# A decoder trunk on one core: the attention scores of a head group in one run, and two chunks of the output projection woven by K blocks

## The chip, the cores and the metric

The kernel runs on one core of a Trainium2 chip. The core has a matrix engine (TensorE, PE in the profile; its weight loads are PEld), VectorE (DVE), ScalarE (ACT), GpSimd (POOL) and SyncE (SP), which here issues most of the DMAs. Each engine works through its own list of instructions, and semaphores make one wait for another. The metric is the device time of one execution in microseconds (us), the median of several runs.

## What is computed

Two layers over 256 tokens with 2048 channels in float32: a Mamba-2 mixer and a SwiGLU network, then differential attention and a second SwiGLU network. The change is in the attention alone. For each of 16 heads there are two score matrices from 64 channels each; their softmaxes are subtracted, the result weighs the values, and the weighted rows are normalized (the sub-norm):

```python
s = jnp.einsum('bhcqd,bhcsd->bhcqs', q_blk, k).astype(jnp.float32)
s = jnp.where(key_pos[None, :] <= q_pos[:, None], s, -jnp.inf)
pr = jax.nn.softmax(s, axis=-1)
pr = pr[:, :, 0] - lam * pr[:, :, 1]
return jnp.einsum('bhqs,bhsd->bqhd', pr.astype(v.dtype), v)
...
o = rmsnorm(o, subln_w) * (1.0 - lambda_init)
return o.reshape(bsz, s_len, D_MODEL) @ w_out
```

## The kernel before

The 256 tokens are two blocks of 128 (t = 0 and 1). Every large product runs on float32 operands split in two parts: a rounded part (hi) and the rest (lo), and three matmuls hi·hi, hi·lo, lo·hi are summed in PSUM. Weights come in blocks of 512 by 512 (1 MB) by DMA from SP into three buffers; `prep` (L130) makes hi by a cast on ACT (L137) and lo by a subtraction on DVE (L138), into four buffers each. So a block's weights can only be split when the block four before it has been used by PE.

Two forms of product occur here. `mv` (L181) holds the activations in the array and streams the weights: for a chunk of 512 output columns it takes four K blocks, each in two halves; a half gives six matmuls for block t = 0 at once and six for t = 1 a little later (they wait in a list, `lag` halves deep). After each half it calls `tick` (L166). `ws` (L205) holds the weights and gives transposed outputs; it is used for queries and keys, and ticks as well.

Small work is put between these products by `later(k, fn)` (L159): fn is emitted at the k-th tick from now. So the work of attention for one head group runs inside the products of the next one. The emitted instructions are then put in an order for each engine by a scheduler, which may move an instruction past others; what it made of both kernels is shown with the change.

`attention_group` (L982) runs for four groups of four heads. It projects the values with `mv`, queries and keys with `ws`. The evacuation `qk_evac` adds two PSUM parts on ACT (L1004) and DVE (L1005), and scales the keys by the norm (L1008, DVE); a key or query tile of 128 columns by two heads is called qk. Then it puts seven pieces of work in the list: three softmaxes (block 0 with all four heads; block 1 with heads 0 and 1; block 1 with heads 2 and 3), three turns (transposes of the weights, L1052, tile pp, copied to prT), and two weightings (L1063, tile po), and last the pieces: two sets of transposes (tile pt_o) that make the operand of the output projection.

A softmax begins with its scores (L1025): for each head one matmul for each half c of 64 rows, into the PSUM tiles sc0 and sc1. They come from the pool aux, which has four banks. DVE masks the diagonal part (L1030), takes the maximum (L1032) and scales it (L1033); ACT takes the exponentials and their sums (L1036, tile e); DVE then divides: a reciprocal (L1038), e1 by its sum times -lambda (L1040), and e0 by its sum plus that (L1042). The weighting squares its rows on ACT (L1067), sums them (L1069, DVE), adds epsilon (L94, DVE), takes the power -1/2 on POOL (L97) and scales the rows (L1071, DVE, tile ob).

`out_proj` (L686) multiplies by the output weights, four chunks n of 512 columns with `mv`; K block k of each chunk needs head group k. `lookup` (L171) empties the list of put-off work when a group's rows are asked for that aren't there yet. PSUM sums (tile acc) come from a second pool with four banks.

Of the kernel before, what the change touches and what calls it, by code (L numbers as in the profile page):

```python
# [10 lines left out]
F32 = mybir.dt.float32  # L11
F32R = mybir.dt.float32r
AF = mybir.ActivationFunctionType
ALU = mybir.AluOpType
AX = mybir.AxisListType

P = 128
# [8 lines left out]
EPS = 1e-6  # L26
# [4 lines left out]
LAG2 = 2  # L31
# [14 lines left out]
def trunk_kernel(ctx, tc, x_rows, x_cols, vec_cols, vec64, post_rows, lam_rows,  # L46
# [19 lines left out]
    def aux(name):  # L66
        return auxp.tile([P, 512], F32, tag="aux", name=name)
# [5 lines left out]
    o = 0  # L73
# [105 lines left out]


    def mv(blocks, stat, evac, lag, scale=None, loaded=()):  # L181
        acc = {}
        last = 2 * len(blocks) - 1

        def run(i, t, hi, lo):
            if i == 0:
                acc[t] = accp.tile([P, 512], F32, tag="acc", name="acc")
            for j in range(2):
                xh, xl = stat(i, j, t)
                for q, (a, b) in enumerate(((xh, hi), (xh, lo), (xl, hi))):  # L190
                    nc.tensor.matmul(acc[t], a, b[:, j], start=(i == 0 and j == 0 and q == 0),  # L191
                                     stop=(i == last and j == 1 and q == 2))
            if i == last:
                evac(t, acc[t])

        for b, src in enumerate(blocks):
            raw = loaded[b] if b < len(loaded) else None
            sc = scale(2 * b) + scale(2 * b + 1) if scale else None
            for i, (hi, lo) in enumerate(halves(src, sc, raw), 2 * b):
                run(i, 0, hi, lo)  # L200
                pending.append(lambda i=i, hi=hi, lo=lo: run(i, 1, hi, lo))
                flush(lag)
                tick()

# [478 lines left out]
        if not final:  # L683
            later(5, stats)

    def out_proj(w, first, last, acts, kgs, step, final, lag, t512, pw, scale=None, ns=range(4), two={}, forms=None, md=None, mid=None):  # L686

        def sums(t, n):
            mt = m[(t, n)]
            row_sumsq(ss4[t][:, n:n + 1], mt, t512("junk"))
            dst = t512("mw") if n == 3 else mt
            (nc.vector if n == 3 else nc.gpsimd).tensor_tensor(dst, mt, pw(n), op=ALU.mult)
            return dst

        up = sorted(kgs)

        def stat(kg, j, t):  # L700
            hi, lo = lookup(acts, (t, kg // 2))
            return hi[:, kg % 2 * 2 + j], lo[:, kg % 2 * 2 + j]

        def up_stat(i, j, t):
            return stat(up[i], j, t)

        def row(t, e):
            if t not in ss4:
                ss4[t] = small.tile([P, 4], F32, tag="ss4", name="ss_m", bufs=3)
            if e not in summed[t]:  # L710
                summed[t].add(e)
                return sums(t, e)

        ss4 = {}
        summed = {t: set() for t in range(NT)}
        if last:
            pw(0)
            if two:
                pw(1)
        for n, seven in two.items():  # L720
            def done(t, c, ps, ss, n=n):
                y, op = ss[(t, c)]
                k = (t, n + 1 - c)
                nc.vector.tensor_tensor(y, ps, y, op=op)  # L724

                dst = None if last else md[t][:, (n + 1 - c) * 512:(n + 2 - c) * 512]
                if last:
                    nc.vector.tensor_tensor(m[k], m[k], y, op=ALU.add)
                elif first:
                    nc.sync.dma_start(dst, y)  # L730
                else:
                    nc.gpsimd.dma_start(dst, y, accum_op=ALU.add)

            pair([[w[n + e, kg // 2][:, kg % 2 * 2:kg % 2 * 2 + 2] for e in range(2)] for kg in kgs],
                 lambda i, j, t: stat(kgs[i], j, t), [kgs.index(kg) for kg in seven], lambda i, f: form_of(lookup(forms, kgs[i]), f), done)
            if last:
                for e in (0, 1):
                    later(4 + e, lambda e=n + e: [row(t, e) for t in range(NT)])
        if mid:
            mid()  # L740
        for n in ns:
            if last:
                if n == 2 and 0 not in ns:

                    later(6, lambda: pw(2))
                else:
                    pw(n)

            def evac(t, ps, n=n):
                if first:  # L750
                    if n == 0:
                        m_tile(t)
                    nc.scalar.copy(m[(t, n)], ps)
                else:
                    nc.vector.tensor_tensor(m[(t, n)], m[(t, n)], ps, op=ALU.add)
                if not last:
                    return
                for e in range(n):
                    row(t, e)
                dst = row(t, n)  # L760
                if n == 2:
                    p3 = small.tile([P, 1], F32, tag="ss1", name="p3", bufs=3)
                    nc.vector.tensor_reduce(p3, ss4[t][:, 0:3], axis=AX.X, op=ALU.add)
                    nc.vector.tensor_scalar(ss4[t][:, 0:1], p3, 1.0 / D, EPS, op0=ALU.mult, op1=ALU.add)
                if n == 3:
                    norm_chain(t, ss4[t], dst, step, final, t512)


            mv([w[n, kg // 2] for kg in up[::2]], up_stat, evac, LAG if last and n == 3 else lag,
               (lambda i: [scale[:, 2 * up[i] + j:2 * up[i] + j + 1] for j in range(2)]) if scale is not None else None)  # L770

# [210 lines left out]
    def attention_group(hg):  # L982
# [28 lines left out]
            ws([w_qkv[4 * which + hg, k] for k in range(4)],  # L1011
               lambda ct, ps, pl, which=which: qk_evac(which, ct, ps, pl))

        prT, es, sms = {}, {}, {}

        def softmax(t, hps):

            nk, ts, nh = t + 1, slice(t * P, (t + 1) * P), 2 * len(hps)

            sc = [aux(f"sc{c}")[:, :nh * nk * P].rearrange("p (h k) -> p h k", h=nh) for c in range(2)]  # L1020
            for h in range(nh):
                qT, kT = qk[(0, hps[h // 2])], qk[(1, hps[h // 2])]
                for c in range(2):
                    cp = slice(c * 64, (c + 1) * 64)
                    nc.tensor.matmul(sc[c][:, h], qT[cp, h % 2, ts], kT[cp, h % 2, :nk * P], start=True, stop=True)  # L1025
            mx = small.tile([P, 2, 4], F32, tag="mx", name="mx", bufs=4)[:, :, :nh]
            sm = small.tile([P, 2, 4], F32, tag="sm", name="sm", bufs=4)[:, :, :nh]
            e = []
            for c in range(2):
                nc.vector.tensor_tensor(sc[c][:, :, ts], sc[c][:, :, ts],  # L1030
                                        causal.unsqueeze(1).to_broadcast([P, nh, P]), op=ALU.add)
                nc.vector.tensor_reduce(mx[:, c], sc[c], axis=AX.X, op=ALU.max)  # L1032
                nc.vector.tensor_scalar(mx[:, c], mx[:, c], qsc[t], -1.0, op0=ALU.mult, op1=ALU.mult)  # L1033
                e.append(t512("e", (P, nh, nk * P)))
                for h in range(nh):
                    nc.scalar.activation(e[c][:, h], sc[c][:, h], AF.Exp, scale=qsc[t], bias=mx[:, c, h:h + 1],  # L1036
                                         accum_out=sm[:, c, h:h + 1])
            nc.vector.reciprocal(sm, sm)  # L1038
            for h in range(nh):
                nc.vector.tensor_scalar(e[1][:, h], e[1][:, h], sm[:, 1, h:h + 1], neglam,  # L1040
                                        op0=ALU.mult, op1=ALU.mult)
                nc.vector.scalar_tensor_tensor(e[0][:, h], e[0][:, h], sm[:, 0, h:h + 1], e[1][:, h],  # L1042
                                               op0=ALU.mult, op1=ALU.add)
            for i, hp in enumerate(hps):
                es[(t, hp)] = e[0][:, 2 * i:2 * i + 2]

# [11 lines left out]
        def weigh(t):  # L1058
# [8 lines left out]
            nc.scalar.activation(ob, po3, AF.Square)  # L1067
            ss = small.tile([P, 4], F32, tag="sso", name="sso", bufs=2)
            nc.vector.tensor_reduce(ss, ob, axis=AX.X, op=ALU.add)  # L1069
            ro = rstd_of(ss, P, f"o{hg}_{t}")  # L1070
            nc.vector.tensor_tensor(ob, po3, ro.unsqueeze(2).to_broadcast([P, 4, P]), op=ALU.mult)  # L1071
            es[t] = ob

        def piece(t):
            att[(t, hg)] = act_piece(es[t].rearrange("p h d -> p (h d)"), f"o{hg}_{t}", scale=subc)

        later(2, lambda: softmax(0, (0, 1)))
        later(3, lambda: softmax(1, (0,)))
        later(4, lambda: softmax(1, (1,)))
        later(5, lambda: turn(0, (0, 1)))  # L1080
        later(6, lambda: (turn(1, (0,)), weigh(0)))
        later(7, lambda: turn(1, (1,)))
        later(8, lambda: weigh(1))
        later(10, lambda: (piece(0), piece(1)))

    for hg in range(4):
        attention_group(hg)
    out_proj(w_ao, True, True, att, list(range(8)), 2, False, LAG2, t512, load_post(2))
    ffn(w_g1, w_u1, w_d1, 3, True)
    flush()  # L1090

# [59 lines left out]
```

## Time and profile before

| | |
|---|---|
| median of 3 runs | 2516.05 us (2515.91 to 2516.57) |
| the profiled execution | 2516.78 us, of which the profile's span is 2514.8 us |
| DMA | 541 MB, 215 GB/s on average |
| granted TensorE clock | 0.999 of full speed |

A row of the page or of the timeline reads: line, engine, operation, written tile <- read tiles, shape; in the timeline the first two columns are the start and the length in us, xN says that N instructions are merged, and the bracket gives idle time of the engine before the row and what ended it. In a group's row the figures behind the bar are busy time and mean ns of one, then idle time. Head group 0's scores lie at 1471 us, those of the others at 1549, 1626 and 1704; the output projection begins at about 1701.

### The profile page before, as it was taken

To read this page: it belongs to the slowest core of one execution; us is meant where nothing else is said; L and a number is where in the kernel's file an instruction comes from. 1 tells how busy PE (TensorE), PEld (TensorE's weight loads), DVE (VectorE), ACT (ScalarE), POOL (GpSimd) and SP (SyncE) were. 2 spreads that over 40 slices of the span, in tenths; PEclk is the share of its full clock that TensorE was granted. 3 is DMA by queue.
4 is the path that set the end of the run, shared out by engine and by line. 5 is a ranking of instruction groups with operands and counts; after the bars stand their busy time and mean duration, and the time that the engine had idled before them with its cause. 6 is when DMAs were issued, how large, how long until landed. Compare 5 with 4: busy or idle time off the path is not lost.

```text
span 2514.8 us, 31507 instructions
## 1 busy us (share of the span) xinstructions
PE 2498.4 (99%) x11818; PEld 2061.9 (82%) x11818; DVE 1942.9 (77%) x2402; ACT 1404.4 (56%) x1895; POOL 264.4 (11%) x242
## 2 busy tenths in 40 slices
PE   9999999999999999999999999999999999999998
PEld 8888888888888888888888888887888888888886
DVE  6877547777688899978987766556688899879985
ACT  5767546666565455555554654455655465546553
POOL 0131001121110010011001100001100100020002
PEclk9999999999999999999999999999999999999999
DMA  7555555555786786778676544544676967687774
GB/s 287 194 174 195 184 198 187 184 175 196 253 277 198 249 260 210 251 221 256 216 253 230 192 165 157 180 163 151 241 233 206 295 215 233 219 267 223 229 245 152
DMA packets 143385, 541.43 MB, mean 215 GB/s; under 512 B 14400, under 2 KB 31104, under 8 KB 116224
## 3 DMA queue, kind: packets, MB, share of 16 engines
q1 hardware_dynamic: 125872, 503.96, 57.9%
q0 software_dynamic: 16992, 35.13, 7.0%
q8 instruction: 93, 1.52, 0.2%
q14 instruction: 60, 0.49, 0.1%
q10 hardware_dynamic: 368, 0.32, 0.1%
HBM read 520.41 MB, written 18.94 MB: 214 GB/s over the span
## 4 chain that ended last, share of the span: by engine, by line
PE 95%; DVE 2%; issue 1%; ACT 1%; DMA 1%; POOL 0%; SPq 0%; DVEq 0%; POOLq 0%; ACTq 0%
PE acc L242 39%; PE acc L191 35%; PE cp L242 9%; PE acc L216 5%; PE acc L218 2%; PE pt_f L303 1%; DVE lo L138 1%; PE sc L1025 1%; PE py L584 1%; PE ptx L665 0%; PE po L1063 0%; PE pc L486 0%; ACT hi L137 0%; PE px L571 0%; PE pt_s L303 0%
## 5 line engine op out<-in xcount | busy, mean ns | idle before, releaser
L138 DVE TENSOR_TENSOR lo<-raw,hi 128x2048 fp32r<-128x2048 f32 (+2 forms) x401 | 729.6, 1823 | 312.3 <-ACT hi L137 303.1
L137 ACT CAST hi<-raw 128x2048 fp32r<-128x2048 f32 (+2 forms) x401 | 604.9, 1510 | 439.9 <-PE acc L191 126.1
L191 PE MATMUL acc<-hi,xT 128*128 128x512 f32 x1792 | 573.6, 395 | 0.0
L242 PE MATMUL acc<-hi,xT 128*128 128x512 f32 x1608 | 518.7, 390 | 0.0
L191 PEld LDWEIGHTS acc<-hi,xT 128*128 128x128 f32 x1792 | 335.6, 188 | 72.5 <-issue 3.2
L191 PE MATMUL acc<-lo,xT 128*128 128x512 f32 x896 | 352.3, 394 | 1.4 <-DVE lo L138 1.4
L242 PEld LDWEIGHTS acc<-hi,xT 128*128 128x128 f32 x1608 | 301.8, 188 | 63.0 <-DVE sx L724 0.3
L242 PE MATMUL acc<-lo,xT 128*128 128x512 f32 x804 | 312.9, 389 | 0.0
L138 DVE TENSOR_TENSOR lo<-rawm,hi 128x2048 fp32r<-128x2048 f32 (+1 forms) x87 | 181.9, 2090 | 35.0 <-ACT hi L137 33.7
L137 ACT CAST hi<-rawm 128x2048 fp32r<-128x2048 f32 (+1 forms) x87 | 152.7, 1756 | 95.7 <-PE acc L242 58.3
L191 PEld LDWEIGHTS acc<-lo,xT 128*128 128x128 f32 x896 | 168.4, 188 | 37.0 <-DVE lo L138 4.9
L216 PE MATMUL acc<-xT,hi 128*128 128x512 f32 x512 | 180.4, 397 | 0.0
L242 PEld LDWEIGHTS acc<-lo,xT 128*128 128x128 f32 x804 | 151.0, 188 | 31.2
L242 PE MATMUL acc<-hi,ah_f 128*128 128x512 f32 x450 | 176.1, 391 | 0.0
L242 PE MATMUL acc<-hi,al_f 128*128 128x512 f32 x450 | 175.2, 389 | 0.0
L242 PE MATMUL acc<-lo,ah_f 128*128 128x512 f32 x450 | 175.1, 389 | 0.0
L242 PE MATMUL cp<-sh,ff 128*128 128x512 f32 x516 | 172.8, 389 | 0.0
L218 PE MATMUL acc<-xT,lo 128*128 128x256 f32 x512 | 143.0, 281 | 0.0
L142 DVE SCALAR_TENSOR_TENSOR lo<-raw,cols,hi 128x512 fp32r<-128x512 f32 x128 | 93.2, 772 | 56.6 <-ACT hi L141 56.1
L141 ACT ACTIVATE hi<-raw,cols 128x512 fp32r<-128x512 f32 x128 | 84.7, 716 | 63.5 <-PE acc L191 42.1
L216 PEld LDWEIGHTS acc<-xT,hi 128*128 128x128 f32 x512 | 96.1, 188 | 22.8
L275 DVE TENSOR_TENSOR sl<-raw,sh 128x1536 fp32r<-128x1536 f32 x54 | 94.9, 1758 | 23.9 <-ACT sh L272 21.4
(298 smaller groups left out, 4097.2 us busy)
## 6 DMA issues: line engine op xcount, KB each, us to landing
raw<-in_w_zxbc_dram SPq DMA_DIRECT2D x77, 1024.0 KB, 4.8
raw<-in_w_d_dram SPq DMA_DIRECT2D x98, 512.0 KB, 5.9
raw<-in_w_g_dram SPq DMA_DIRECT2D x96, 512.0 KB, 6.4
raw<-in_w_u_dram SPq DMA_DIRECT2D x96, 512.0 KB, 6.2
raw<-in_w_qkv_dram SPq DMA_DIRECT2D x48, 1024.0 KB, 4.8
raw<-in_w_so_dram SPq DMA_DIRECT2D x32, 1024.0 KB, 4.8
rawm<-in_w_g_dram SPq DMA_DIRECT2D x64, 512.0 KB, 5.8
rawm<-in_w_u_dram SPq DMA_DIRECT2D x64, 512.0 KB, 6.2
```

The source lines that it names most:

```text
L137: nc.scalar.copy(hi, raw)
L138: nc.vector.tensor_tensor(lo, raw, hi.bitcast(F32), op=ALU.subtract)
L141: nc.scalar.activation(hi[:, j], raw[:, j], AF.Copy, scale=scale[j])
L142: nc.vector.scalar_tensor_tensor(lo[:, j], raw[:, j], scale[j], hi[:, j].bitcast(F32), op0=ALU.mult, op1=ALU.subtract)
L191: nc.tensor.matmul(acc[t], a, b[:, j], start=(i == 0 and j == 0 and q == 0), stop=(i == last and j == 1 and q == 2))
L216: nc.tensor.matmul(acc[ct], hi[:, j, cs], x.rearrange("p a s -> p (a s)"), start=(i == 0 and j == 0), stop=False)
L218: nc.tensor.matmul(acc[ct][:, :S], lo[:, j, cs], x[:, 0], start=False, stop=(i == last and j == 1))
L242: nc.tensor.matmul(acc[k], a, b, start=first and q == 0, stop=last and q == 2)
L275: nc.vector.tensor_tensor(sl[:, 0:3], raw[:, 0:3], sh[:, 0:3].bitcast(F32), op=ALU.subtract)
L303: nc.tensor.transpose(pt[:, j], src[:, j * P:(j + 1) * P], ident)
L584: nc.tensor.matmul(py[e * 64:(e + 1) * 64, a], xd[c][:, 2 * a + e], mts[c][:, 2 * a + e], start=True, stop=True)
L1025: nc.tensor.matmul(sc[c][:, h], qT[cp, h % 2, ts], kT[cp, h % 2, :nk * P], start=True, stop=True)
```

## The change

Four things are changed.

1. `mv` becomes a special case of `mvs`, which takes several chunks and an order of (chunk, block) pairs. The output projection of attention weaves its first two chunks: blocks 0, 1, 2 of chunk 0, then 0, 1, 2 of chunk 1, then block 3 of both.
2. The scores of all three softmaxes of a group are emitted in one run, in the second tick: block 1 heads 0 and 1, block 0 all heads, block 1 heads 2 and 3. The tiles of block 0 come from the pool of acc instead of aux.
3. e0 is no longer divided by its sum s0. The weights become e0 - lambda (s0/s1) e1, one operation a head, and since rows s0 times as large are normalized afterwards, the sub-norm adds epsilon times s0 squared (the tile eps) instead of epsilon.
4. Turns, weightings and pieces come at later ticks (6, 8, 10, 11, 13 instead of 5, 6, 7, 8, 10).

```diff
     def mv(blocks, stat, evac, lag, scale=None, loaded=()):
+        mvs([(blocks, evac)], [(0, b) for b in range(len(blocks))], stat, lag, scale, loaded)
+
+    def mvs(jobs, order, stat, lag, scale=None, loaded=()):
         acc = {}
...
-        for b, src in enumerate(blocks):
+        for job, b in order:
...
+            if weave and n < 2:
+                woven.append(([w[n, kg // 2] for kg in up[::2]], evac))
+                if n:
+                    mvs(woven, [(0, 0), (0, 1), (0, 2), (1, 0), (1, 1), (1, 2), (0, 3), (1, 3)], up_stat, lag)
+                continue
...
-            sc = [aux(f"sc{c}")[:, :nh * nk * P].rearrange("p (h k) -> p h k", h=nh) for c in range(2)]
+            banks = [aux(f"sc{c}") if t else accp.tile([P, 512], F32, tag="acc", name=f"sc{c}") for c in range(2)]
+            sc = [b[:, :nh * nk * P].rearrange("p (h k) -> p h k", h=nh) for b in banks]
...
-            nc.vector.reciprocal(sm, sm)
+            rs = small.tile([P, 4], F32, tag="rsm", name="rsm", bufs=4)[:, :nh]
+            nc.vector.reciprocal(rs, sm[:, 1])
+            nc.vector.scalar_tensor_tensor(rs, sm[:, 0], neglam, rs, op0=ALU.mult, op1=ALU.mult)
             for h in range(nh):
-                nc.vector.tensor_scalar(e[1][:, h], e[1][:, h], sm[:, 1, h:h + 1], neglam,
-                                        op0=ALU.mult, op1=ALU.mult)
-                nc.vector.scalar_tensor_tensor(e[0][:, h], e[0][:, h], sm[:, 0, h:h + 1], e[1][:, h],
+                nc.vector.scalar_tensor_tensor(e[0][:, h], e[1][:, h], rs[:, h:h + 1], e[0][:, h],
                                                op0=ALU.mult, op1=ALU.add)
+            if t not in eps_s:
+                eps_s[t] = small.tile([P, 4], F32, tag="eps", name="eps", bufs=4)
+            nc.vector.scalar_tensor_tensor(eps_s[t][:, 2 * hps[0]:2 * hps[0] + nh], sm[:, 0], EPS, sm[:, 0],
+                                           op0=ALU.mult, op1=ALU.mult)
...
-            ro = rstd_of(ss, P, f"o{hg}_{t}")
+            nc.vector.scalar_tensor_tensor(ss, ss, 1.0 / P, eps_s[t], op0=ALU.mult, op1=ALU.add)
+            ro = small.tile([P, 4], F32, tag="rs4", name="ro", bufs=6)
+            nc.gpsimd.tensor_tensor(ro, ss, mhalf.to_broadcast([P, 4]), op=ALU.pow)
...
+        def all_scores():
+            b = scores(1, (0,))
+            a = scores(0, (0, 1))
+            c = scores(1, (1,))
+            for x in (a, b, c):
+                softmax(*x)
+
+        later(2, all_scores)
+        later(6, lambda: turn(0, (0, 1)))
+        later(8, lambda: (turn(1, (0,)), weigh(0)))
+        later(10, lambda: turn(1, (1,)))
+        later(11, lambda: weigh(1))
+        later(13, lambda: (piece(0), piece(1)))
...
-    out_proj(w_ao, True, True, att, list(range(8)), 2, False, LAG2, t512, load_post(2))
+    out_proj(w_ao, True, True, att, list(range(8)), 2, False, LAG2, t512, load_post(2), weave=True)
```

The lists of the engines follow, as they stand in the built programs. First PE in head group 0, before, from the third of the block 0 scores on (qk_12058 is the key tile of heads 0 and 1, qk_12073 that of heads 2 and 3; xT is the activation that the next value projection holds):

```order
L1025 MATMUL sc0_12103<-qk_12073,qk_11905 128x128
L1025 MATMUL sc1_12104<-qk_12073,qk_11905 128x128
L191 MATMUL acc_12090<-hi357_12142,xT1_100 128x512
L191 MATMUL acc_12090<-lo357_12143,xT1_100 128x512
L191 MATMUL acc_12090<-hi357_12142,xT1_100 128x512 x2
L191 MATMUL acc_12090<-lo357_12143,xT1_100 128x512
L1025 MATMUL sc0_12103<-qk_12073,qk_11905 128x128
L1025 MATMUL sc1_12104<-qk_12073,qk_11905 128x128
L191 MATMUL acc_12090<-hi357_12142,xT1_100 128x512
```

The same place of PE now, from the second head of block 0 on:

```order
L1038 MATMUL sc0_12109<-qk_12058,qk_11892 128x128
L1038 MATMUL sc1_12110<-qk_12058,qk_11892 128x128
L1038 MATMUL sc0_12109<-qk_12073,qk_11905 128x128
L1038 MATMUL sc1_12110<-qk_12073,qk_11905 128x128
L1038 MATMUL sc0_12109<-qk_12073,qk_11905 128x128
L1038 MATMUL sc1_12110<-qk_12073,qk_11905 128x128
L1038 MATMUL sc0_12119<-qk_12073,qk_11905 128x256
L1038 MATMUL sc1_12120<-qk_12073,qk_11905 128x256
L1038 MATMUL sc0_12119<-qk_12073,qk_11905 128x256
L1038 MATMUL sc1_12120<-qk_12073,qk_11905 128x256
L197 MATMUL acc_12090<-hi357_12195,xT1_100 128x512
```

Five projection matmuls stood between the third and the fourth head of block 0; now all sixteen score matmuls of the group stand together, four of 256 columns ahead of these rows, and 48 projection matmuls follow before the first turn.

Next DVE at that place before (the weight split, the last key tile's addition and scaling, then the masks):

```order
L138 TENSOR_TENSOR lo359_12282<-raw_12279,hi359_12281 128x2048
L1005 TENSOR_TENSOR qk_12073<-qk_12073,acc_11917 128x256
L1008 TENSOR_TENSOR qk_12073<-qk_12073,rstd_bc_105 128x256
L1030 TENSOR_TENSOR sc0_12103<-sc0_12103,causal_11474 128x512
L1030 TENSOR_TENSOR sc1_12104<-sc1_12104,causal_11474 128x512
```

And DVE now (the lines have shifted by 13 to 18):

```order
L138 TENSOR_TENSOR lo359_12264<-raw_12261,hi359_12263 128x2048
L1018 TENSOR_TENSOR qk_12073<-qk_12073,acc_11917 128x256
L1048 TENSOR_TENSOR sc0_12103<-sc0_12103,causal_11474 128x2x128
L1021 TENSOR_TENSOR qk_12073<-qk_12073,rstd_bc_105 128x256
L1048 TENSOR_TENSOR sc1_12104<-sc1_12104,causal_11474 128x2x128
```

The first mask of block 1 has moved between the addition and the scaling of the last key tile. It stands so in all four groups.

Third, PE in the output projection before, from the last weighting of group 3 on (hi396, hi397 are blocks of chunk 1, and hi395 is the last block of chunk 0):

```order
L1063 MATMUL po_14151<-v_13548,prT_14149 128x128 x4
L191 MATMUL acc_14225<-lo396_14222,ah_o0_0_12396 128x512
L191 MATMUL acc_14225<-hi397_14258,al_o1_0_13016 128x512
L303 MATMUL pt_o3_0_14169<-ident_86,ob_14129 128x128 x4
L191 MATMUL acc_14268<-hi396_14221,ah_o0_1_12405 128x512
L303 MATMUL pt_o3_1_14178<-ident_86,ob_14160 128x128 x4
L191 MATMUL acc_14268<-lo396_14222,ah_o0_1_12405 128x512
L191 MATMUL acc_13949<-hi395_14140,ah_o3_0_14174 128x512
```

And PE there now (hi398 is the last block of chunk 0, hi399 that of chunk 1):

```order
L1085 MATMUL po_14232<-v_13525,prT_14212 128x128 x4
L197 MATMUL acc_14131<-hi397_14216,ah_o2_0_13697 128x512
L197 MATMUL acc_14188<-hi396_14178,al_o1_1_13087 128x512
L309 MATMUL pt_o3_0_14267<-ident_86,ob_14168 128x128 x4
L309 MATMUL pt_o3_1_14276<-ident_86,ob_14241 128x128 x4
L197 MATMUL acc_14188<-hi397_14216,ah_o2_1_13706 128x512
L197 MATMUL acc_13954<-hi398_14263,ah_o3_0_14272 128x512
L197 MATMUL acc_14131<-hi399_14317,ah_o3_0_14272 128x512
```

Of the projection matmuls between weighting and transposes only some rows stand here: there are 11 before and 12 now. The two sets of transposes now follow each other, and eight more projection matmuls stand behind them before the first that needs them.

More of the change, by code (lines that the diff above doesn't have):

```diff
@@ L181, in mv, with run @@
     def mv(blocks, stat, evac, lag, scale=None, loaded=()):
+        mvs([(blocks, evac)], [(0, b) for b in range(len(blocks))], stat, lag, scale, loaded)
+    def mvs(jobs, order, stat, lag, scale=None, loaded=()):
         acc = {}
-        last = 2 * len(blocks) - 1
-        def run(i, t, hi, lo):
+        def run(job, i, t, hi, lo):
+            blocks, evac = jobs[job]
+            last = 2 * len(blocks) - 1
             if i == 0:
-                acc[t] = accp.tile([P, 512], F32, tag="acc", name="acc")
+                acc[job, t] = accp.tile([P, 512], F32, tag="acc", name="acc")
             for j in range(2):
@@ L190, in run @@
                 for q, (a, b) in enumerate(((xh, hi), (xh, lo), (xl, hi))):
-                    nc.tensor.matmul(acc[t], a, b[:, j], start=(i == 0 and j == 0 and q == 0),
+                    nc.tensor.matmul(acc[job, t], a, b[:, j], start=(i == 0 and j == 0 and q == 0),
                                      stop=(i == last and j == 1 and q == 2))
             if i == last:
-                evac(t, acc[t])
-        for b, src in enumerate(blocks):
+                evac(t, acc[job, t])
+        for job, b in order:
             raw = loaded[b] if b < len(loaded) else None
             sc = scale(2 * b) + scale(2 * b + 1) if scale else None
-            for i, (hi, lo) in enumerate(halves(src, sc, raw), 2 * b):
-                run(i, 0, hi, lo)
-                pending.append(lambda i=i, hi=hi, lo=lo: run(i, 1, hi, lo))
+            for i, (hi, lo) in enumerate(halves(jobs[job][0][b], sc, raw), 2 * b):
+                run(job, i, 0, hi, lo)
+                pending.append(lambda job=job, i=i, hi=hi, lo=lo: run(job, i, 1, hi, lo))
                 flush(lag)
@@ L684, in norm_chain, with out_proj @@
             later(5, stats)
-    def out_proj(w, first, last, acts, kgs, step, final, lag, t512, pw, scale=None, ns=range(4), two={}, forms=None, md=None, mid=None):
+    def out_proj(w, first, last, acts, kgs, step, final, lag, t512, pw, scale=None, ns=range(4), two={}, forms=None, md=None, mid=None,
+                 weave=False):
         def sums(t, n):
@@ L740, in out_proj @@
             mid()
+        woven = []
         for n in ns:
@@ L1012, in attention_group, with scores @@
                lambda ct, ps, pl, which=which: qk_evac(which, ct, ps, pl))
-        prT, es, sms = {}, {}, {}
-        def softmax(t, hps):
+        prT, es, eps_s = {}, {}, {}
+        def scores(t, hps):
             nk, ts, nh = t + 1, slice(t * P, (t + 1) * P), 2 * len(hps)
-            sc = [aux(f"sc{c}")[:, :nh * nk * P].rearrange("p (h k) -> p h k", h=nh) for c in range(2)]
+            banks = [aux(f"sc{c}") if t else accp.tile([P, 512], F32, tag="acc", name=f"sc{c}") for c in range(2)]
+            sc = [b[:, :nh * nk * P].rearrange("p (h k) -> p h k", h=nh) for b in banks]
             for h in range(nh):
@@ L1025, in softmax @@
                     nc.tensor.matmul(sc[c][:, h], qT[cp, h % 2, ts], kT[cp, h % 2, :nk * P], start=True, stop=True)
+            return t, hps, sc
+        def softmax(t, hps, sc):
+            nk, ts, nh = t + 1, slice(t * P, (t + 1) * P), 2 * len(hps)
             mx = small.tile([P, 2, 4], F32, tag="mx", name="mx", bufs=4)[:, :, :nh]
@@ L1075, in piece @@
             att[(t, hg)] = act_piece(es[t].rearrange("p h d -> p (h d)"), f"o{hg}_{t}", scale=subc)
[L1077 to L1084, printed above, removed]
+        def all_scores():
[10 more added lines that the diff above has]
+        later(13, lambda: (piece(0), piece(1)))
     for hg in range(4):
         attention_group(hg)
-    out_proj(w_ao, True, True, att, list(range(8)), 2, False, LAG2, t512, load_post(2))
+    out_proj(w_ao, True, True, att, list(range(8)), 2, False, LAG2, t512, load_post(2), weave=True)
     ffn(w_g1, w_u1, w_d1, 3, True)
```

## The prediction, made before the changed kernel was run

> **What bounds the kernel now.** I read the page first: the busy shares, then the chain that ended last.
>
> ```profile
> PE 2498.4 (99%) x11818; PEld 2061.9 (82%) x11818; DVE 1942.9 (77%) x2402; ACT 1404.4 (56%) x1895; POOL 264.4 (11%) x242
> PE 95%; DVE 2%; issue 1%; ACT 1%; DMA 1%; POOL 0%; SPq 0%; DVEq 0%; POOLq 0%; ACTq 0%
> ```
>
> TensorE (PE) is the bound almost everywhere: 95% of the chain is its own work. An edit that takes work from VectorE (DVE) or ScalarE (ACT) is worth nothing by itself; an edit is worth what it takes out of PE's stream in pauses and in badly packed matmuls. So I looked at the two places that the change rearranges, matmul by matmul. First the stretch from 1418 to 1800 us (attention and its output projection), by windows (columns: length, then busy time of each engine with its count, granted clock, DMA share, GB/s).
>
> ```profile
> core 0: us, PE busy (x) PEld busy (x) DVE busy (x) ACT busy (x) POOL busy (x), PEclk, DMA share, GB/s
> 1418.00:1800.00 382.00, 380.20 (x2034) 315.13 (x2033) 230.83 (x306) 190.48 (x285) 20.88 (x15) 1.00 0.50 173
> ```
>
> Only 1.8 us of 382 are open idleness, so idle time alone understates what can be won: a busy span also covers a matmul that started late and drained alone. What counts is the step from one start to the next. In PE's timeline of head group 0 a projection matmul follows the last after 0.23 us:
>
> ```profile
> 1471.09 0.39 PE L191 MATMUL acc<-lo,xT 128*128 128x512 f32 x1
> 1471.31 0.39 PE L191 MATMUL acc<-hi,xT 128*128 128x512 f32 x1
> 1471.63 0.94 PE L1025 MATMUL sc<-qk 64*128 64x128 f32 x12
> 1472.50 0.50 PE L191 MATMUL acc<-hi,xT 128*128 128x512 f32 x1
> 1472.84 0.39 PE L191 MATMUL acc<-lo,xT 128*128 128x512 f32 x1
> ```
>
> Twelve score instructions (six matmuls, two passes each; the pairs for the two 64-row halves run together, so six steps) take the slot from 1471.54 (last projection start plus 0.23) to 1472.61 (second one after, less 0.23): 1.07 us. The same reckoning gives the four score bursts of this group; the windows of the score tile alone are cut at these slots:
>
> ```profile
> 1471.54:1472.61 1.07, 0.94 (x12) 0.75 (x12) 0.00 (x0) 0.00 (x0) 1.00 0.04 15
> 1473.76:1474.45 0.69, 0.49 (x4) 0.30 (x4) 0.01 (x1) 0.00 (x0) 1.00 1.24 190
> 1476.06:1477.32 1.26, 1.13 (x8) 0.69 (x8) 0.87 (x3) 0.16 (x1) 1.00 0.88 364
> 1480.07:1482.01 1.94, 1.82 (x8) 0.97 (x8) 0.00 (x0) 1.94 (x9) 1.00 0.02 4
> sum 4.96, PE 4.38 PEld 2.71 DVE 0.88 ACT 2.10; mean PE 1.09 PEld 0.68 DVE 0.22 ACT 0.52
> ```
>
> So scores cost PE 4.96 us a group. Two of the bursts hold a wait, seen on the weight loads:
>
> ```profile
> 1473.53 0.40 PE L191 MATMUL acc<-lo,xT 128*128 128x512 f32 x1
> 1473.92 0.30 PEld L1025 LDWEIGHTS sc<-qk 64*128 64x128 f32 x4 [0.43 <-DVE qk L1008]
> 1480.85 0.51 PEld L1025 LDWEIGHTS sc<-qk 64*128 64x128 f32 x5 [0.39 <-ACT e L1036]
> ```
>
> In the second burst the start comes 0.39 us after the projection matmul at 1473.53 instead of the 0.32 of burst 1: it waited 0.07. With a fixed cost c of a burst, a of a 128-column step and b of a 256-column step: 1.07 = c + 6a and 0.62 = c + 2a give a = 0.11 and c = 0.40; 1.26 = c + 4b gives b = 0.215. The fourth burst should then be 1.26 too; it is 1.94, so 0.68 went to waiting for exponentials to free PSUM banks.
>
> **The change, part by part.** *Scores in one run.* The work is 8a + 8b = 2.63 us; with one c it is 3.03, against 4.96. The bank wait goes, since the first block's scores now sit in the projection's pool. That would be 1.93 us a group, but what is late next? The order shows it: the scores stand unbroken, those of the fourth head of block 0 in their middle, and these need the key tile that L1008 scales last. Before, five projection matmuls filled that time. And on DVE a mask now stands ahead of that scaling.
>
> ```profile
> 1470.79 2.29 DVE L138 TENSOR_TENSOR lo<-raw,hi 128x2048 fp32r<-128x2048 f32 x1 [1.03 <-ACT hi L137]
> 1472.99 0.41 DVE L1005 TENSOR_TENSOR qk<-qk,acc 128x256 f32<-128x256 f32 x1
> 1473.44 0.42 DVE L1008 TENSOR_TENSOR qk<-qk,rstd_bc 128x256 f32<-128x256 f32 x1
> 1477.32 0.77 DVE L1030 TENSOR_TENSOR sc<-sc,causal 128x256 f32<-128x256 f32 x2
> ```
>
> PE reaches the waiting pair at 1471.63 + 0.10 (entry) + 4b + 6a = 1473.27 on this clock. The key let the score start at 1473.92. One mask (0.77 for two, so 0.36 to 0.41) stands between; some of it fits into the 0.04 us that DVE waits for itself, so 0.27 to 0.41 is added: start at 1474.19 to 1474.33. I take 1474.25: a pause of 0.98, and 0.10 to refill. Behind the waiting scores stand the second pair's scores and the whole projection. The burst becomes 3.03 + 1.08 = 4.11, a gain of 0.85 a group, 3.4 for four. Group 2 had one more bank wait, which goes as well:
>
> ```profile
> PE sc L1025 <- ACT e L1036: 0.3, 1, 0.3
> ```
>
> Term: **3.7 us**. Ends: 8.0 if no pause comes (4 x 1.93 + 0.3), and nothing if the pause grows to 1.9.
>
> The Trainium skill, TensorE: Matmul & The Clock Gate, section "Architectural detail: the array is 16× 32×32, not 1× 128×128", says that VectorE and ScalarE work strictly first in, first out, and that on TensorE only weight loads are pulled ahead. It speaks against this change: by it neither the scaling can pass the mask nor the ready scores pass the waiting one, and the sum stays with 3.7; could they pass, it would be 8.0. The trace agrees so far: at 1473.92 PE waited although ready projection matmuls stood next.
>
> *The shorter weighting.* The added factor and epsilon operations and the removed 128-column scalings lie on DVE; before, its first turn of block 0 waited for none of them, and by the order 48 projection matmuls (10.9 us) now stand between the scores and the first turn. I cost them at nothing. If that cover went, PE would wait in each group for what is left of the block's eight exponentials, 3.5 us at most (rows under the slower rival).
>
> *Output projection.* Before, PE waits for the normalized rows of the last group:
>
> ```profile
> 1730.92 0.39 PE L191 MATMUL acc<-hi,al_o 128*128 128x512 f32 x1
> 1732.14 0.66 PE L303 MATMUL pt_o<-ident,ob 128*128 128x128 f32 x4 [0.84 <-DVE ob L1071]
> 1732.56 0.48 PE L191 MATMUL acc<-hi,ah_o 128*128 128x512 f32 x1
> 1733.12 0.66 PE L303 MATMUL pt_o<-ident,ob 128*128 128x128 f32 x4
> 1728.82 0.60 ACT L1067 ACTIVATE ob<-po 128x512 f32<-128x512 f32 x1 [1.25 <-PE po L1063]
> 1729.45 0.69 DVE L1069 TENSOR_REDUCE sso<-ob 128x4 f32<-128x512 f32 x1 [0.19 <-ACT ob L1067]
> 1730.05 0.29 DVE L94 TENSOR_SCALAR ms_o<-sso 128x4 f32<-128x4 f32 x2
> 1730.36 1.98 POOL L97 TENSOR_TENSOR rs_o<-ms_o,mhalf 128x4 f32<-128x4 f32 x2 [73.52 <-DVE ms_o L94]
> 1732.37 0.69 DVE L1071 TENSOR_TENSOR ob<-po,rs_o 128x512 f32<-128x512 f32 x1 [0.28 <-POOL rs_o L97]
> ```
>
> The first wait is 1732.14 - 1731.15 = 0.99, the second 1733.12 - 1732.56 - 0.32 = 0.24: 1.2 us. In the order of the change 12 projection matmuls (2.7 us) and the first block's transposes (0.4) stand between the last weighting and the second transposes. The chain there is square 0.60, reduction 0.69, one small operation 0.2, power about 1.0, scaling 0.69 and some 0.3 for hand-overs: 3.5. So 0.35 of waiting is left, **0.9 us** gained; ends 1.2, and -0.4 if a weight split slips ahead of the reduction, as one of 2.3 us does in these rows' neighbourhood.
>
> The weave itself adds no matmul, and the order before already drew blocks of chunk 1 ahead. The load of the second row of weights moves ahead of this projection's weight loads; it is 0.25 MB among loads of 1 MB, the buffers that it waits for are long read, and I cost it at nothing.
>
> *Fewer breaks.* After a break the projection matmuls keep a longer step for a while; the first and last of eleven behind a turn:
>
> ```profile
> 1717.78 0.40 PE L191 MATMUL acc<-lo,ah_o 128*128 128x512 f32 x1
> 1720.09 0.39 PE L191 MATMUL acc<-hi,al_o 128*128 128x512 f32 x1
> ```
>
> Ten steps take 2.31 us, 0.231 each, against the 0.22 to 0.23 of the start rows at 1471 (0.227 taken): about 0.04 us a break. A group had ten breaks (four of scores, three turns, two weightings, the pieces) and has six: 16 x 0.04 = **0.6 us**.
>
> *The rhythm of the key and query projections.* Their pairs run in two rhythms in this trace; the rows are the page's, a quiet stretch's (1436 to 1450) and a late one's (1662 to 1700).
>
> ```profile
> L216 PE MATMUL acc<-xT,hi 128*128 128x512 f32 x512 | 180.4, 397 | 0.0
> L216 PE MATMUL acc<-xT,hi 128*128 128x512 f32 x42 | 14.6, 391 | 0.0
> L216 PE MATMUL acc<-xT,hi 128*128 128x512 f32 x108 | 38.1, 399 | 0.0
> ```
>
> Turns now break into these projections and may set either rhythm: 512 x 6 ns = 3.1 us to win, 512 x 2 ns = 1.0 to lose. The row nearest is the page's own mean, so I take zero.
>
> **Sum**: 3.7 + 0.9 + 0.6 = 5.2 us. The profiled execution took 2516.78 us around its span of 2514.8, 0.7 above the median of 2516.05; the difference goes onto the median: **2510.8 us**. A measurement of this kernel tells about 0.2% (5.0 us) from no change, so the forecast lies at that edge.
>
> **The rivals.** *No pause* (the key ready in time): 8.0 + 0.9 + 0.6 = 9.5, 2506.5 us. For it: only 0.65 us have to vanish without the mask. Against it: the mask stands ahead of the scaling on DVE in every group. *The pause eats the gain*: PE waits some 1.9 us, because masks and scores hold each other up further; 1 to 2.5 us are left, 2514.2 us. For it: every engine's queue is now one block of softmax. This is also the case that the change does little of what it says.
>
> *Slower*: the weight blocks starve. All sixteen exponentials of a group now precede the next ACT cast, and all of the softmax the next DVE split:
>
> ```profile
> 1477.16 0.46 ACT L1036 ACTIVATE e<-sc,mx,qsc 128x128 f32<-128x128 f32 x1 [6.14 <-DVE mx L1033]
> 1480.66 0.59 ACT L1036 ACTIVATE e<-sc,mx,qsc 128x256 f32<-128x256 f32 x1
> 1482.83 1.95 ACT L137 CAST hi<-raw 128x2048 fp32r<-128x2048 f32 x1
> 1486.65 2.28 DVE L138 TENSOR_TENSOR lo<-raw,hi 128x2048 fp32r<-128x2048 f32 x1
> ```
>
> Eight short ones take 3.50 and four long ones 2.17, so sixteen take 7.8 us. From the start of the scores the cast would end near 15.7 us and the split near 17.6. The query projection needs it after 96 matmuls, turns and scores, at about 25; the output projection, its fifth block at about 22. It decides from a slip of 5 to 7 us; to be slower by 5.0 in all, four groups must each lose (5.2 + 5.0)/4 = 2.6 us more than that. It would give 2521 us. Against it: nothing in the trace stretches a softmax so far.
>
> **How the numbers follow.** Forecast 0.58 (2509.0 to 2512.6), no pause 0.14, pause eats the gain 0.22, slower 0.06. Of the forecast's case 0.36 lies beyond 0.2% and 0.22 within; so faster 0.50, same 0.44, slower 0.06. The range, 2506.3 to 2514.2, holds the forecast's case, half of either neighbour, and little of the last: about 0.8.
>
> **What would show it.** Right: one score burst a group of about 4.1 us with a wait on the scaled key of 0.9 to 1.0 inside; no wait of scores for exponentials; one wait of about 0.35 at the last transposes. Wrong: a burst near 3.0 or near 5.0; a projection matmul that waits for a cast or a split; turns that wait for exponentials; the pairs of L216 (by its new line) all in one rhythm.

## The result, and the profile after

| | median, us | against before |
|---|---|---|
| before | 2516.05 (2515.89 to 2516.57) | |
| after | 2538.51 (2538.27 to 2538.93) | ratio 1.0089 [1.0078, 1.0101] |
| predicted | 2510.8 (2506.3 to 2514.2) | |

The change makes the kernel 22.5 us slower. The page of after shows the same number of matmuls as before, PE as busy and as much of the chain as before, only for longer:

```profile
PE 2518.6 (99%) x11818; PEld 2066.1 (81%) x11818; DVE 1939.9 (76%) x2394; ACT 1402.6 (55%) x1895; POOL 261.4 (10%) x242
PE 96%; DVE 1%; ACT 1%; issue 1%; DMA 0%; POOL 0%; SPq 0%; DVEq 0%; ACTq 0%; POOLq 0%
```

PE is 20.2 us busier (2498.4 before), its idle time grew by 1.6 us only (span less busy time: 16.4 to 18.0), no engine has taken its place, and the granted clock is 0.999 in both. So the loss is neither a starved weight block nor a new wait. Where the time went is read by comparing the same instructions in both programs. Two small sets of matmuls lie well for this: one at the beginning of attention (tile pb, the row before the first key scaling) and one behind its output projection (tile pt_f). The views of one tile give their first and last starts; first before:

```profile
L324 PE MATMUL pb<-dg,ones x4: 270/274/275, 1423.5 to 1423.9; 128*128 128x128 f32 x4
L303 PE MATMUL pt_f<-ident,g x8: 271/272/328, 1846.4 to 1852.0; 128*128 128x128 f32 x8
```

and after:

```profile
L330 PE MATMUL pb<-dg,ones x4: 272/275/275, 1442.2 to 1442.6; 128*128 128x128 f32 x4
L309 PE MATMUL pt_f<-ident,g x8: 272/272/273, 1859.0 to 1864.7; 128*128 128x128 f32 x8
```

After is 18.7 us late at the first place, although PE's 6659 matmuls up to there come in the same order in both traces. It then gains 6.1 us through attention (12.6 late at the second), and loses 9.2 more by the end (spans 2514.8 and 2536.6), where the order is again the same. So 27.9 us are lost in code whose matmuls the change left alone. There the groups of the page separate. Before:

```profile
L242 PE MATMUL acc<-hi,xT 128*128 128x512 f32 x1608 | 518.7, 390 | 0.0
L242 PE MATMUL acc<-hi,ah_f 128*128 128x512 f32 x450 | 176.1, 391 | 0.0
```

After:

```profile
L248 PE MATMUL acc<-hi,xT 128*128 128x512 f32 x1608 | 526.8, 395 | 0.0
L248 PE MATMUL acc<-hi,ah_f 128*128 128x512 f32 x450 | 176.2, 392 | 0.0
```

The matmuls that hold xT in the array have become longer; those of the same line that hold ah_f have not. Their durations overlap, so I take the step from start to start, in PE's timeline of a quiet stretch of the first SwiGLU network. Before, nine steps from the first lo to the last:

```profile
801.11 0.39 PE L242 MATMUL acc<-lo,xT 128*128 128x512 f32 x1
801.34 0.62 PE L242 MATMUL acc<-hi,xT 128*128 128x512 f32 x2
...
803.15 0.39 PE L242 MATMUL acc<-lo,xT 128*128 128x512 f32 x1
```

After, the same number:

```profile
801.28 0.40 PE L248 MATMUL acc<-lo,xT 128*128 128x512 f32 x1
801.51 0.62 PE L248 MATMUL acc<-hi,xT 128*128 128x512 f32 x2
...
803.37 0.39 PE L248 MATMUL acc<-lo,xT 128*128 128x512 f32 x1
```

2.04 us for nine steps became 2.09: 0.227 us a step against 0.232, with no wait in either. The page's four largest groups count 1792 + 896 + 1608 + 804 = 5100 matmuls of hi or lo with xT; at 5.5 ns more each that is 28 us. Smaller groups (tiles cp, sh and sl) hold 408 more with xT, which would add 2.

**The theory.** What differs for these matmuls, if not their order, is where their operands lie in SBUF. The addresses in the two built programs show it. The change adds the tags rsm and eps to the pool `small` and drops one (ms4, the epsilon's sum in `rstd_of`), each four buffers of 32 B a partition: 128 B more. `small` stands ahead of the pools of activations (ah, al) and weights (raw, hi, lo), but behind `const`, which holds xT. So all of the former moved up by 128 B, and xT did not:

| tile, first buffer | before | after |
|---|---|---|
| xT | 18944 | 18944 |
| ah | 71168 | 71296 |
| hi | 128512 | 128640 |
| lo | 144896 | 145024 |

Before, all four addresses are multiples of 512 B. After, the distance of hi and lo to xT is 128 B off that; their distance to ah is not. Theory A: this distance lengthens the step. Rival B: the new order, or what VectorE and ScalarE now do, slows PE. The rival has against it that slow steps lie where PE's order is the same, but only a run can decide.

### The profile page after: what moved, and what is told of

The parts are those of the page before. It is cut to its first block, busy times and chain, and to the rows that moved or that the text cites. A ratio compares the mean times of both kernels' runs of the same rounds, so it can differ in the third digit from the quotient of the medians.

```text
span 2536.6 us, 31493 instructions
## 1 busy us (share of the span) xinstructions
PE 2518.6 (99%) x11818; PEld 2066.1 (81%) x11818; DVE 1939.9 (76%) x2394; ACT 1402.6 (55%) x1895; POOL 261.4 (10%) x242
## 4 chain that ended last, share of the span: by engine, by line
PE 96%; DVE 1%; ACT 1%; issue 1%; DMA 0%; POOL 0%; SPq 0%; DVEq 0%; ACTq 0%; POOLq 0%
PE acc L248 39%; PE acc L197 36%; PE cp L248 9%; PE acc L222 5%; PE acc L224 2%; DVE lo L138 1%; PE pt_f L309 1%; PE py L590 1%; ACT hi L137 1%; PE ptx L671 0%; PE po L1085 0%; PE pc L492 0%; PE pt_s L309 0%; PE px L577 0%; DMA mt<-acum_d 0%
## 5 line engine op out<-in xcount | busy, mean ns | idle before, releaser
L197 PE MATMUL acc<-hi,xT 128*128 128x512 f32 x1792 | 578.9, 398 | 0.6 <-ACT hi L137 0.6
L248 PE MATMUL acc<-hi,xT 128*128 128x512 f32 x1608 | 526.8, 395 | 0.0
L197 PE MATMUL acc<-lo,xT 128*128 128x512 f32 x896 | 355.4, 397 | 1.2 <-DVE lo L138 1.2
L248 PE MATMUL acc<-lo,xT 128*128 128x512 f32 x804 | 317.2, 395 | 0.0
L222 PE MATMUL acc<-xT,hi 128*128 128x512 f32 x512 | 180.7, 395 | 0.0
L224 PE MATMUL acc<-xT,lo 128*128 128x256 f32 x512 | 144.0, 283 | 0.0
L248 PEld LDWEIGHTS cp<-sh,ff 128*128 128x128 f32 x516 | 96.9, 188 | 21.0
```

The source lines that it names most:

```text
L197: nc.tensor.matmul(acc[job, t], a, b[:, j], start=(i == 0 and j == 0 and q == 0), stop=(i == last and j == 1 and q == 2))
L222: nc.tensor.matmul(acc[ct], hi[:, j, cs], x.rearrange("p a s -> p (a s)"), start=(i == 0 and j == 0), stop=False)
L224: nc.tensor.matmul(acc[ct][:, :S], lo[:, j, cs], x[:, 0], start=False, stop=(i == last and j == 1))
L248: nc.tensor.matmul(acc[k], a, b, start=first and q == 0, stop=last and q == 2)
```

## The experiments

### The layout alone, in both directions

The kernel has two padding tiles: gap1 stands between `small` and the pools that moved, gap0 ahead of xT. The changed kernel with its layout restored:

```diff
-    gap1 = gapp.tile([P, 40], F32, name="gap1")
+    gap1 = gapp.tile([P, 8], F32, name="gap1")
```

> The changed kernel with the padding tile gap1 128 B smaller per partition (40 to 8 elements), so that every tile behind it, the split weights among them, stands at the address that it has in the kernel before. Instructions and order stay those of the change. Theory A (the two tags that the change adds to the pool small, less the one that goes, move the split weights hi and lo by 128 B against xT, and that lengthens the step of the matmuls on xT from 227 to 231-232 ns): the 18.4 us lost by 1411 us and the 9 us lost after 1808 us go, and the 5.8 us gained between stay: 2509 to 2512 us; the hi,xT group of the gate and up projections again at 390 ns. Rival B (the other order of instructions, or the softmax work on VectorE and ScalarE, slows TensorE): nothing changes, 2538 us.

The kernel before, with the layout of the change:

```diff
-    gap1 = gapp.tile([P, 40], F32, name="gap1")
+    gap1 = gapp.tile([P, 72], F32, name="gap1")
```

> The kernel before with gap1 128 B larger per partition (40 to 72 elements), so that every tile behind it stands where the change puts it; not one instruction of the computation differs. Theory A: slower by the 18.4 + 9 us that the change lost outside attention, 2540 to 2546 us. Rival B: 2516 us.

The changed kernel with xT moved along, so that the distance is that of before and the place is not:

```diff
-    gap1 = gapp.tile([P, 40], F32, name="gap1")
+    gap1 = gapp.tile([P, 8], F32, name="gap1")
...
-    gap0 = const.tile([P, 88], F32, name="gap0")
+    gap0 = const.tile([P, 120], F32, name="gap0")
```

> The changed kernel with gap1 128 B smaller and the padding tile gap0, ahead of xT, 128 B larger (88 to 120 elements): xT and the split weights both stand 128 B above their places in the kernel before, so their distance is that of before and the absolute places of the weights are those of the change. Theory A in the form that the distance between the two operands decides: 2509 to 2512 us. Theory A in the form that the weights' own place decides: 2538 us. Rival B: 2538 us.

Half of the shift (gap1 of 24 elements), and later twice the shift (72 elements):

> The changed kernel with gap1 64 B smaller (40 to 24 elements): the split weights stand 64 B above their places of before, half of the change's shift. Theory A gives no number by itself: 2524 us if the loss grows evenly with the shift, 2510 or 2538 us if it is a matter of which residue the distance falls on. Rival B: 2538 us.

> The changed kernel with gap1 128 B larger (40 to 72 elements): the split weights stand 256 B above their places in the kernel before, twice the change's shift. If the distance counts only by its remainder to 256 B, as the bare matmuls show (227 ns at 256, 233 at 128 and 384): 2509.4 us as with no shift. If a larger shift costs as much or more, 2538 us and above.

| weights moved against xT by | kernel | us | ratio to before |
|---|---|---|---|
| 0 | after, gap1 smaller | 2509.43 | 0.9971 [0.9960, 0.9983] |
| 0, both 128 B up | after, both gaps | 2509.63 | 0.9972 [0.9962, 0.9982] |
| 64 B | after, gap1 smaller | 2520.29 | 1.0014 [1.0004, 1.0023] |
| 128 B | after | 2538.51 | 1.0089 [1.0078, 1.0101] |
| 128 B | before, gap1 larger | 2544.67 | 1.0111 [1.0096, 1.0126] |
| 256 B | after, gap1 larger | 2509.64 | 0.9973 [0.9963, 0.9983] |

Padding alone makes the kernel before 27.9 us slower (its median beside these runs was 2516.76, and 2516.05 beside the first ones, so that differences of under 1 us between sets of runs say nothing), and takes 29.1 us from the changed one. Rival B falls: not an instruction of the computation differs within either pair. The distance decides and not the place (second row), and its size alone does not: 256 B cost nothing. Growth in proportion to the shift would have put the 64 B run at 2524, and a plain hit or miss at 2510 or 2538; it came out at 2520.3. The page of the first of these runs has the groups of before again:

```profile
L248 PE MATMUL acc<-hi,xT 128*128 128x512 f32 x1608 | 518.6, 390 | 0.0
L222 PE MATMUL acc<-xT,hi 128*128 128x512 f32 x512 | 180.9, 398 | 0.0
```

### The distance by itself

To see the distance apart from the kernel, one execution of bare matmuls: 48 in a row for each pair of starts, the stationary operand at s bytes into its tile and the moving one at m bytes into its own (the two tiles themselves lie at the same remainder to 512 B). The core of its code:

```python
for k in range(16):
    for q, (s, m) in enumerate(((0, mva), (0, mvb), (256, mva))):
        nc.tensor.matmul(acc, sta[:, s0 + s:s0 + s + P], m[:, m0:m0 + 512],
                         start=k == 0 and q == 0, stop=k == 15 and q == 2)
```

> Not the reference's computation: all of it is left out, and the output holds no result. 48 matmuls of 128 rows by 512 columns in a row for each of 19 pairs of start addresses of the stationary and the moving operand, in the kernel's order hi, lo, hi; five of them again with VectorE and ScalarE busy beside. If the distance of the two operands alone lengthens the step: 227 ns where both start at the same residue of 512 B (0/0, 0/512, 0/1024, 128/128), 231 to 232 ns at 0/128 and 128/0, some 229 ns at 0/64. If the place of the moving operand alone decides: 128/128 as slow as 0/128, and 128/0 as fast as 0/0. If it needs other engines at work in the same memory: 227 ns in every series with TensorE alone, and 231 to 232 ns only in the series with work beside.

The views of one tile show the lengths (least, median, most) and the first and last starts; five of the series, at 0/0, 0/128, 0/64, 0/256 and 128/128:

```profile
L73 PE MATMUL acc_a<-mva,sta x32: 389/389/389, 32.5 to 43.1; 128*128 128x512 f32 x32
L73 PE MATMUL acc_b<-mva,sta x32: 392/394/398, 43.3 to 54.3; 128*128 128x512 f32 x32
L73 PE MATMUL acc_c<-mva,sta x32: 392/393/397, 54.5 to 65.3; 128*128 128x512 f32 x32
L73 PE MATMUL acc_d<-mva,sta x32: 389/389/398, 65.5 to 76.2; 128*128 128x512 f32 x32
L73 PE MATMUL acc_e<-mva,sta x32: 389/389/396, 76.5 to 87.1; 128*128 128x512 f32 x32
```

Of the 48 matmuls, 47 steps lie between the first and the last start: 10.6 us (a) or 11.0 (b). From the starts to the nanosecond, the first five steps of each series left out (in a fast series behind a slow one they can still be long: 224 to 236 ns in d):

| distance moving less stationary, B | s/m of the series | mean step, ns |
|---|---|---|
| a multiple of 256 | 0/0, 128/128, 0/256, 256/0, 0/512, 512/0, 0/1024 | 226.7 to 227.3 |
| 64 past one | 0/64, 0/320, 64/128 | 228.9 |
| 128 past one | 0/128, 0/384, 128/0 | 232.4 to 233.3 |
| 32, 96 or 192 past one | 0/32, 0/96, 0/192, 0/448 | 233.3 to 233.5 |
| 32 short of one | 32/0 | 233.3 |
| 16 past one | 0/16 | 231.6 |

The second set of the five shown was meant to have VectorE and ScalarE busy beside. It had not: their work waited for nothing in these series, and ran early, beside the first ones. The windows of 0/0 and 0/128, first set and then second (columns as in the prediction's windows):

```profile
32.50:43.10 10.60, 10.60 (x48) 8.78 (x47) 10.46 (x7) 10.41 (x7) 0.00 (x0) 1.00 0.00 0
43.30:54.30 11.00, 11.00 (x49) 8.83 (x48) 10.51 (x6) 3.02 (x2) 0.00 (x0) 1.00 0.00 0
242.40:253.10 10.70, 10.70 (x49) 8.83 (x48) 0.16 (x1) 0.00 (x0) 0.00 (x0) 1.00 0.00 0
253.30:264.20 10.90, 10.90 (x48) 8.81 (x47) 0.16 (x1) 0.00 (x0) 0.00 (x0) 1.00 0.01 2
```

So the comparison is there with the sets exchanged. 0/0 took 226.7 ns with both engines at work and 227.1 alone; 0/128 took 233.3 both with VectorE at work (ScalarE for 3.0 of 11 us) and alone. All other slow series ran alone as well, so the longer step needs no other engine. The kernel's own steps agree: between successive matmuls with xT, from 740 to 1380 us, the mean is 226.9 ns with no shift and at 256 B, 229.0 at 64 B and 232.6 at 128 B. At 64 B the 2.1 ns more, for 5508 matmuls, are 11.6 us; that run lies 10.9 us above the one with no shift.

### One step later, and the weave alone

With the layout restored, each burst of scores still waits 0.7 us for the key, as predicted in kind. The scores one step later:

```diff
-        later(2, all_scores)
+        later(3, all_scores)
```

> The changed kernel with gap1 128 B smaller (as in the run that gave 2509.4 us) and the score burst of each group one step later in the program's order (three instead of two), so that the key's last scaling is ready when its scores come. If the 0.69 us that each burst waits for L1021 is a wait that only moves with the burst, 4 x (0.69 + about 0.09 of refill) = 3.1 us go: 2506.3 us, burst at 3.2 us. If the masks and the weight splits then hold up something else (the first turn waiting for block 0's exponentials, a projection matmul waiting for a split), the gain is smaller: 2508 to 2511 us, with a wait of a turn or of a projection in its place.

2506.50 us (2506.22 to 2507.03), ratio 0.9961 [0.9948, 0.9975]: the wait is gone, and no wait of a turn or of a projection took its place. The timeline of head group 0 in this run:

```profile
1474.10 0.43 DVE L1021 TENSOR_TENSOR qk<-qk,rstd_bc 128x256 f32<-128x256 f32 x1
...
1474.69 0.39 PE L197 MATMUL acc<-hi,xT 128*128 128x512 f32 x1
...
1475.01 2.89 PE L1038 MATMUL sc<-qk 64*128 64x256 f32 x32
...
1477.83 0.50 PE L197 MATMUL acc<-hi,xT 128*128 128x512 f32 x1
1478.17 0.40 PE L197 MATMUL acc<-lo,xT 128*128 128x512 f32 x1
```

The key's scaling ends at 1474.53, 0.48 us ahead of the burst; all 32 score instructions stand unbroken, and by the prediction's reckoning the burst costs 3.02 us. The four bursts together are 3.9 us shorter than with the wait, and attention, from tile pb to tile pt_f in the two profiled executions, 3.7. The median fell by 2.9 (3.1 expected); in the profiled execution the stretch ahead of attention, which this edit leaves alone, was 0.7 us longer. This version is 0.4% faster than the kernel before.

The other part by itself, the kernel before with nothing but the woven projection:

```diff
-    out_proj(w_ao, True, True, att, list(range(8)), 2, False, LAG2, t512, load_post(2))
+    out_proj(w_ao, True, True, att, list(range(8)), 2, False, LAG2, t512, load_post(2), weave=True)
```

> The kernel before with nothing but the woven order of the output projection's first two chunks; attention and its tiles are those of before, so no tile moves. If the weave by itself brings what the changed kernel shows there (the last transposes cost 1.41 us instead of 2.58), 1.2 us go: 1.2 below the kernel before of the same call, 2515.5 us. If the shorter wait needs the change's other order of weightings (turns and weightings of the last group set apart), the wait stays and the time is that of before within 0.3 us.

2514.91 us against 2516.16, ratio 0.9995 [0.9986, 1.0004]: the time alone can't tell it from no change. The profile can. Its last transposes, in PE's timeline:

```profile
1734.96 0.40 PE L197 MATMUL acc<-hi,al_o 128*128 128x512 f32 x1
1735.20 1.04 PE L309 MATMUL pt_o<-ident,ob 128*128 128x128 f32 x8
1735.99 0.47 PE L197 MATMUL acc<-hi,ah_o 128*128 128x512 f32 x1
1736.31 0.40 PE L197 MATMUL acc<-lo,ah_o 128*128 128x512 f32 x1
```

Both sets run as one without a wait, from 1735.19 to 1736.08 (last start plus 0.23, second one after less 0.23): 0.89 us. In the kernel before they begin behind the projection matmul at 1730.92, and two more projection matmuls follow the second set:

```profile
1733.53 0.48 PE L191 MATMUL acc<-lo,ah_o 128*128 128x512 f32 x1
1733.85 0.40 PE L191 MATMUL acc<-hi,ah_o 128*128 128x512 f32 x1
```

From 1731.15 to 1733.62, less 0.23 for the one projection matmul between the sets, they cost 2.24 us. (The 2.58 of the expectation is the sum of two slots that overlap and both hold that matmul.) So the weave alone takes 1.35 us out here, close to the 1.25 by which the medians differ, and it doesn't need the change's other ticks; with them a wait of 0.31 us is left (below) that it doesn't have alone.

## Why the prediction was wrong

**The step that failed** is the frame of the sum. It held that an edit "is worth what it takes out of PE's stream in pauses and in badly packed matmuls", so every matmul outside attention was taken to keep its length without a term for it. Of the "added factor and epsilon operations" it says "I cost them at nothing". Their time is indeed hidden: no turn stands in PE's list of waits. What was not counted is that their results need two new tags in a pool ahead of the weights, which moves one operand of 5508 matmuls by 128 B against the other. This term of 29.1 us (2538.51 - 2509.43) has no place among the forecast's terms or its rivals, and it is larger than all the terms together. The slower rival, starved weight blocks, was right in sign by luck and wrong in mechanism: PE's list of waits for after (us in total, times, longest) has only this for splits and casts, over the whole kernel:

```profile
PE acc L197 <- DVE lo L138: 1.2, 4, 0.5
PE acc L197 <- ACT hi L137: 0.6, 1, 0.6
```

**The rest of the sum** can be read from the run with the layout restored, 7.3 us below before (2516.76 to 2509.43) where 5.2 was predicted. Its tile views give, at the two places of above:

```profile
L330 PE MATMUL pb<-dg,ones x4: 270/274/275, 1423.5 to 1423.8; 128*128 128x128 f32 x4
L309 PE MATMUL pt_f<-ident,g x8: 270/272/328, 1839.1 to 1844.7; 128*128 128x128 f32 x8
```

Level with before at 1423.5, and 7.3 us ahead at 1839.1: all of the gain lies in attention, as argued. (In the changed kernel itself this gain was only 6.1, since 1.2 us of the loss fell inside attention.)

*Scores.* Predicted 3.7. The burst of after, head group 0, in the timeline:

```profile
1490.17 0.40 PE L197 MATMUL acc<-hi,xT 128*128 128x512 f32 x1
1490.50 1.80 PE L1038 MATMUL sc<-qk 64*128 64x256 f32 x20
1491.84 0.41 DVE L1018 TENSOR_TENSOR qk<-qk,acc 128x256 f32<-128x256 f32 x1
1492.17 0.42 DVE L1048 TENSOR_TENSOR sc<-sc,causal 128x256 f32<-128x256 f32 x1
1492.51 0.41 DVE L1021 TENSOR_TENSOR qk<-qk,rstd_bc 128x256 f32<-128x256 f32 x1
1492.97 1.36 PE L1038 MATMUL sc<-qk 64*128 64x128 f32 x12 [0.67 <-DVE qk L1021]
1494.26 0.50 PE L197 MATMUL acc<-hi,xT 128*128 128x512 f32 x1
1494.60 0.39 PE L197 MATMUL acc<-lo,xT 128*128 128x512 f32 x1
```

From 1490.40 to 1494.37 is 3.97, where 4.11 was predicted. The mechanism was right, the pause a little too long. PE could have started the pair 1.64 us after the burst's start, as predicted: it does so in the run with the scores one step later, where nothing waits. The key let it go after 2.47 us instead of 2.62, since the mask put the scaling off by 0.22 us (0.67 from the addition's start to the scaling's, 0.45 before) and not by 0.33. So the pause is 0.83 us, where 0.98 was predicted; the 0.67 in the bracket counts only from the end of the last matmul. Over four groups the layout-restored run gives 16.0 us for the bursts against 20.1 before: 4.1 gained. Ready scores and projection matmuls stood behind the waiting pair, and none went ahead. By the Trainium skill (TensorE: Matmul & The Clock Gate, section "Architectural detail: the array is 16× 32×32, not 1× 128×128") TensorE can pull weight loads ahead of matmuls in flight. The trace agrees in so far as no matmul passed the waiting one, in 0.67 us of idle time.

*Output projection.* Predicted 0.9 with a wait of 0.35 left. In the layout-restored run:

```profile
1734.01 0.39 PE L197 MATMUL acc<-hi,al_o 128*128 128x512 f32 x1
1734.24 0.60 PE L309 MATMUL pt_o<-ident,ob 128*128 128x128 f32 x4
1735.15 0.66 PE L309 MATMUL pt_o<-ident,ob 128*128 128x128 f32 x4 [0.31 <-DVE ob L1095]
1735.56 0.48 PE L197 MATMUL acc<-hi,ah_o 128*128 128x512 f32 x1
1735.88 0.40 PE L197 MATMUL acc<-lo,ah_o 128*128 128x512 f32 x1
```

The wait is 0.31, and the slot is 1.41 us instead of 2.24: 0.8 gained. Mechanism and size were right.

*Fewer breaks.* Predicted 0.6; what is left of 7.3 is 2.4. Reckoned from the starts of all matmuls in both traces, turns and weightings cost 17.2 us in slots before and 15.3 with the layout restored: 1.9 gained, with four of the twelve turns now running straight on into a weighting. The other 0.5 lies outside all slots, where the longer steps behind a break would show; the border between the two is only good to some tenths, since some turns now stand among the key and query projections, whose steps alternate. So the longer steps may well have brought what was predicted, and the term was mis-sized because it left out what the breaks of turns and weightings cost themselves.

*The rhythm of the key and query projections.* Taken as zero, and rightly: L222 has 180.9 us with the layout restored and 180.4 before.

*The rivals.* "No pause" was put 9.5 us below before; the run with the scores one step later came out 9.7 below (2516.16 to 2506.50). Its term for the scores, 8.0, is what their bursts gained there (20.1 to 12.1). So only the place of the scores in the order stood between the two cases. "The pause eats the gain" was wrong: the pause did not grow beyond the forecast's.

## What to carry to other kernels

A new tile is an edit to every tile behind it: before predicting, compare the addresses of the operands of the costliest matmuls in both programs, and, for matmuls like these, keep stationary and moving operands a multiple of 256 B apart (in their start addresses), with padding if need be. When a change is slower than its reasons allow, look first at the stretches that it did not touch: the same instruction's start in both traces, at two or three places, says at once where the time went. A wait on another engine's queue may go by emitting the waiting work a step later, as it did here; a run tells whether another wait takes its place.

## What the runs showed of the hardware that was not expected

The step of a 128 by 512 float32 matmul with its own weights depends on the distance between the starts of its two operands, by the remainder to 256 B in all pairs tried: 227 ns at 0, 228.9 at 64, 231.6 to 233.5 at 16, 32, 96, 128, 192 and 224. Here 128 B cost 1.1% of the whole kernel, while the page showed PE 99% busy, next to no waiting and the full clock in both cases. The pairs of L222 and L224, which hold the weights and stream xT, show no such loss at the same shift. Before, L224's line was L218:

```profile
L218 PE MATMUL acc<-xT,lo 128*128 128x256 f32 x512 | 143.0, 281 | 0.0
```

And after:

```profile
L222 PE MATMUL acc<-xT,hi 128*128 128x512 f32 x512 | 180.7, 395 | 0.0
L224 PE MATMUL acc<-xT,lo 128*128 128x256 f32 x512 | 144.0, 283 | 0.0
```

The former had 180.4 before, and a pair of the two took 352 to 353 ns from start to start in both. Why these are spared, and why the remainder matters, is open. So is a smaller effect: in after, matmuls that hold the tile ff, which moved along with the weights, also went from 226.7 to 228.8 ns a step. They stand among those with xT, and the steps of the bare series d behind a slow one suggest that a slow stretch lengthens the first steps after it; no run here tests that.
